# A decoder layer on one core: row stores on another queue, a reordered overflow job, and a score product of full height

## The chip, the cores and the metric

The kernel runs on one core of a Trainium2 chip. A core has TensorE (PE in the profile, with PEld for its weight loads), VectorE (DVE), ScalarE (ACT), GpSimd (POOL) and SyncE (SP), which computes nothing here and issues DMAs. Each of SP, ACT and POOL issues the DMAs of its own queue in program order; the transfers run on the core's 16 DMA engines. The metric is the time of one launch in device microseconds.

## The reference

The kernel computes one layer of a hybrid decoder trunk for 1024 tokens of width 1024, in float32. Two branches (a gated linear recurrence, and attention with a compressed key and value latent) read one combined projection; they are merged by gates, pass an output product and are added to the residual. Then a router chooses for each token one of eight groups and two of the eight experts in it, and the experts' outputs, weighted, are added to the residual. Cut to the two places that the change touches:

```python
# attention, per head: key and query have 128 plain and 64 rotary dimensions
k = rmsnorm(concat([k_nope, k_pe]), qk_k_g);  q = rmsnorm(q, qk_q_g)
q, k = rope on the last 64 dimensions
for s0 in range(0, 1024, 128):                      # blocks of 128 queries, causal
    s = einsum("bqhd,bkhd->bhqk", q[:, s0:e], k[:, :e]) * scale
    o = softmax(mask(s)) @ v[:, :e]
# experts
h = x + merged @ w_out
expert, gate = top 2 of the experts in the best group of rmsnorm(h) @ router
y[token] += gate * ((silu(u @ w1[e]) * (u @ w3[e])) @ w2[e])     # 64 experts, D_EXPERT 256
out = h + y
```

## The kernel before

The work runs in stages, all on one core: the input products (to about 590 us of the profile), attention by heads (591 to 898), the two branch products and the merge (898 to 985), the output product with the router (985 to 1128), and the experts (1128 to the end).

**Attention.** Products are made from float32 numbers that are split into a high and a low part. `head_T` makes the transposed, split queries and keys of a head (`qnh`, `qnl`, `knh`, `knl` for the 128 plain dimensions; `qpe`, `kph`, `kpl` for the rotary ones), in tiles of two buffers each. In `qpe`, rows 0 to 63 hold the high part of the rotary query and rows 64 to 127 the low part; `kph` holds the rotary key's high part over the same 128 rows; `kpl` holds its low part in rows 0 to 63 alone. `attn_a` makes the scores of one block of 128 queries in groups of five products (L691) into one PSUM bank: `knh` by `qnh`, `knl` by `qnh`, `knh` by `qnl`, `kph` by `qpe`, all of 128 rows, and `kpl` by `qpe` of 64 rows. A block has one group, or two where more than 512 keys are in reach. VectorE then adds the mask and takes the extreme of each row (L695), ScalarE takes the exponential (L700), PE transposes the probabilities (L718) and multiplies them by the values (L119, L120). GpSimd makes the rotated parts of the next head (L625 to L643) and some of the low parts (L116).

**Output product and router.** `product` multiplies one block of 128 tokens by the output weights, which lie split in eight tiles `wo0` to `wo7` (L989). `route` adds the residual, stores the rows to two tensors in memory (`xs_d` at L1009, `out` at L1010; 512 KB each), both issued by SP, makes the router's logits (L1035) and the position of each token in a table, and scatters two sets of rows into that table, `tab_d`, by indirect DMAs of GpSimd (L1123). There are eight blocks. The table holds 128 places for each of 32 tiles, and one load brings it back as `rec_all` (L1156, SP).

**Experts.** A tile `t` is two experts of 64 places each. `gather` fetches its rows from `xs_d` (L1198, GpSimd), `select` transposes them (L1233), `gemm1` makes the two hidden products (L1271), `turn` and `gemm2` the last one (L1284, L1298), `gather_out` and `scatter` add it to `out` (L1216, L1223). The weights come in chunks of 1 MB, six a tile, through a ring of 19 buffers that `wchunk` hands out in order: five `c` and four `m`, which stand on space that is free from the merge on, and ten `w` (`w9` to `w18`), which stand where the output weights and the router's tiles were. `load` issues the chunks on SP (L1247), two tiles ahead. The row indices of tile 0 are made ahead of the table's return (`first_tile`), so its gather waits for no table load.

**The overflow job.** Places beyond an expert's 64 are computed in jobs of one expert and 64 rows. One job is always run among the tiles, as a generator that the tile loop steps on: the first `next(job)` issues three chunks (L1392) and a gather (L1395), the second makes the hidden products (L1405), the third turns them (L1413), the fourth makes the last product (L1424) and the scatter. With `JI = 6` these steps stand in the program at tiles 6, 7, 8 (behind that tile's `load`) and at the end of tile 9. A scheduler may move instructions against the order in which the program is written, within what tiles and buffers allow.

Of the kernel before, what the change touches and what calls it, by code (L numbers as in the profile page):

```python
# [43 lines left out]
JI = 6  # L44
# [7 lines left out]
def block_kernel(ctx, tc, x, positions, norm1_g, w_in, conv_w, conv_b, lru_wa, lru_ba, lru_wx,  # L52
# [3 lines left out]
    nc = tc.nc  # L56
# [502 lines left out]
    with pool_of(name="hd", bufs=2) as hd, \  # L559
# [86 lines left out]
        def head_T(pr, j, hf, which):  # L646
            if ("t", j) not in pr:
                pr["t", j] = {nm: hd.tile([128, S], F32R, name=nm)
                              for nm in ("qnh", "qnl", "knh", "knl", "qpe", "kph", "kpl")}
            t = pr["t", j]  # L650
            qs, ks = pr["qs"], pr["ks"]
            qp, kp = pr["qk", j, hf]
            s_ = slice(hf * 512, hf * 512 + 512)
            pt = tps.tile([128, 4, 128], F32, name="tp")
            for q in range(4):
                tb = hf * 4 + q
                src = (qs[:, tb, j, 0:DN], ks[:, tb, j], qp[:, q].rearrange("p a b -> p (a b)"),
                       kp[:, q].rearrange("p a b -> p (a b)"))[which]
                nc.tensor.transpose(pt[:, q], src, ident)
            pt = pt.rearrange("p a b -> p (a b)")  # L660
            if which < 2:
                a, b = (("qnh", "qnl"), ("knh", "knl"))[which]
                gcol = pch[:, 64 + which:65 + which]
                nc.scalar.activation(t[a][:, s_], pt, AF.Copy, scale=gcol)
                nc.vector.scalar_tensor_tensor(t[b][:, s_], pt, gcol, f32v(t[a][:, s_]),
                                               op0=ALU.mult, op1=ALU.subtract)
            elif which == 2:
                hi_of(t["qpe"][:, s_], pt)
                lo_of(t["qpe"][64:128, s_], pt[64:128], t["qpe"][64:128, s_], nc.vector)
            else:  # L670
                hi_of(t["kph"][:, s_], pt)
                lo_of(t["kpl"][0:64, s_], pt[0:64], t["kph"][0:64, s_], nc.vector)
# [4 lines left out]
        def attn_a(h, qb):  # L677
# [8 lines left out]
            for ch in range(nw):  # L686
                cc = slice(ch * w, ch * w + w)
                for n, (a, b, r) in enumerate((("qnh", "knh", 128), ("qnh", "knl", 128),
                                               ("qnl", "knh", 128), ("qpe", "kph", 128),
                                               ("qpe", "kpl", 64))):  # L690
                    nc.tensor.matmul(psv[:, ch], t[a][0:r, qsl], t[b][0:r, cc],  # L691
                                     start=n == 0, stop=n == 4)

# [252 lines left out]
    with pool_of(name="xe", bufs=1, side="right") as xe, \  # L946
# [45 lines left out]
        def route(tb):  # L992
# [11 lines left out]
            for hf in range(2):  # L1004
# [1 line left out]
                nc.vector.tensor_tensor(xt[:, s_], xt[:, s_], px[:, s_], op=ALU.add)  # L1006
                junk = wo.tile([128, 512], BF16, name="junk", bufs=2)
                nc.scalar.activation(junk, xt[:, s_], AF.Square, accum_out=ss[:, hf:hf + 1])
            nc.sync.dma_start(xs_d[tsl, :], xt)  # L1009
            nc.sync.dma_start(out[tsl, :], xt)  # L1010
            nc.vector.tensor_tensor(ss[:, 0:1], ss[:, 0:1], ss[:, 1:2], op=ALU.add)
            rec = rp.tile([128, 2, 4], F32, name="rec", bufs=4)
            nc.vector.memset(rec, 0.0)
# [106 lines left out]
            for j in range(2):  # L1120
                pos = rp.tile([128, 1], I32, name=f"pos{j}", bufs=4)
                nc.vector.tensor_copy(pos, ps_[:, j:j + 1])
                nc.gpsimd.indirect_dma_start(  # L1123
                    out=tab_d, out_offset=bass.IndirectOffsetOnAxis(ap=pos, axis=0),
                    in_=rec[:, j], in_offset=None, bounds_check=128 * NT_ - 1, oob_is_err=False)

        for tb in range(NB):
            product(tb, 0)
# [7 lines left out]
        for _ in route(NB - 1):  # L1136
# [16 lines left out]
    onef = eg.tile([128, 64], F32, name="onef")  # L1153
    nc.gpsimd.memset(onef, 1.0)
    rec_all = eg.tile([128, NT_, 4], F32, name="rec_all")
    nc.sync.dma_start(rec_all.rearrange("p a c -> p (a c)"),  # L1156
                      tab_d.rearrange("(p a) c -> p (a c)", p=128))
    toki = eg.tile([128, NT_], I32, name="toki")
    nc.vector.tensor_copy(toki, rec_all[:, :, 0])
# [52 lines left out]
    def gather_out(t):  # L1212
        xo = rows_("xo")
        if t < 3:
            nc.gpsimd.memset(xo, 0.0)
        unordered(nc.gpsimd.indirect_dma_start(  # L1216
            out=xo, out_offset=None, in_=out,
            in_offset=bass.IndirectOffsetOnAxis(ap=tok_of(t), axis=0),
            bounds_check=S - 1, oob_is_err=False), t)
        st["xo", t] = xo  # L1220
# [216 lines left out]
    for t in range(NT_):  # L1437
        if t == 1:
            job_table()
            jrec, ji = job_rec(eg, cps, const, "kro")  # L1440
            job = job_run(jrec, ji, eg, wchunk, (cps, hps, tps2, yps), ("c", "ph", "pt", "py"),
                          rows_)
        if t + 2 < NT_:
            gather(t + 2)
        if t:
            gather_out(t - 1)
        if 3 <= t + 2 < NT_ - 1:
            load(t + 2, (w1_r, w3_r, w2_r))
        elif t + 2 == NT_ - 1:
            load(t + 2, (w1_r, w3_r))  # L1450
            for hf in range(2):
                load_2h(t + 2, hf)
        if JI <= t < JI + 3:
            next(job)
        gemm1(t)
        if t + 1 < NT_:
            select(t + 1)
        if t:
            turn(t - 1)
            gemm2(t - 1)  # L1460
            scatter(t - 1)
        if t == JI + 3:

            next(job)
    gather_out(NT_ - 1)
# [51 lines left out]
```

## Time and profile before

| | before |
|---|---|
| median of 3 runs (least to most) | 1696.21 us (1695.99 to 1697.54) |
| profiled execution, whole | 1698.7 us |
| its span | 1696.9 us |
| PE busy | 1527.0 us, 90% |
| DVE, ACT, POOL busy | 715.5, 499.0, 459.7 us |
| read from memory, written | 307.74 MB, 48.59 MB |

The time outside the span is 1.8 us. PE's share of 90% is an average over stages: it is nearly full in the input products, in attention and in the output product, while in the experts' stage the DMA engines are nearly full and PE has gaps. So each stage has to be read by itself, and the views below are all cut by stretch, line or engine. A matmul's duration in the profile is longer than its distance to the next one, since matmuls are pipelined; what a product costs in a row of products is read from the start times.

### The profile page before, as it was taken

How to read it: one execution, taken by the hardware profiler on the slowest of the kernel's cores; microseconds unless marked ns; L12 is line 12 of the kernel's file. 1: busy time of each engine (PE TensorE's matmuls, PEld its weight loads, DVE VectorE, ACT ScalarE, POOL GpSimd, SP SyncE). 2: the span in 40 equal slices, each digit the busy share in tenths (PEclk: the TensorE clock that was granted, in tenths of full speed). 3: DMA queues.
4: the chain of work that ended last, by engine and by line, in shares of the span. 5: the costliest groups of instructions: out<-in, count | busy, mean ns of one | idle time of the engine just before them, and what ended most of it. 6: DMA issues, size and time to landing. Idle time of an engine off the chain costs nothing. (4 is left out here: it accounts for less than half of the span.)

```text
span 1696.9 us, 22297 instructions
## 1 busy us (share of the span) xinstructions
PE 1527.0 (90%) x8484; PEld 1141.5 (67%) x8484; DVE 715.5 (42%) x1806; ACT 499.0 (29%) x1088; POOL 459.7 (27%) x456
## 2 busy tenths in 40 slices
PE   5999998999999999999998999979739879878776
PEld 5988886888888877878777878856416445444443
DVE  7744646420012777777875346644102222112111
ACT  5325464631112466666553112210000000000000
POOL 4034343321223235252603411232200221211111
PEclk9999999999999999999999999989869999999999
DMA  5212212353345201010206674349997999999995
GB/s 189 61 53 64 64 59 62 100 186 100 99 157 168 78 8 38 10 38 25 76 16 212 194 261 161 114 187 417 418 413 295 418 417 417 413 406 412 404 415 199
DMA packets 129489, 331.89 MB, mean 196 GB/s; under 512 B 16315, under 2 KB 81413, under 8 KB 104677
## 3 DMA queue, kind: packets, MB, share of 16 engines
q1 hardware_dynamic: 113844, 304.02, 47.7%
q0 software_dynamic: 14816, 25.57, 4.1%
q8 instruction: 68, 1.11, 0.3%
q10 hardware_dynamic: 720, 0.85, 0.2%
q14 instruction: 41, 0.33, 0.1%
HBM read 307.74 MB, written 48.59 MB: 210 GB/s over the span
## 5 line engine op out<-in xcount | busy, mean ns | idle before, releaser
L116 POOL TENSOR_TENSOR w_lo<-w_raw,w_hi 128x1024 fp32r<-128x1024 f32 x40 | 97.6, 2440 | 266.2 <-ACT w_hi L113 266.1
L1271 PE MATMUL ph<-w,x 128*64 128x256 f32 x992 | 140.2, 395 | 19.6 <-DMA w<-in_exp_w_dram 19.5
L259 PE MATMUL pp<-uTh,w_hi 128*128 128x512 f32 x496 | 156.3, 396 | 1.1 <-ACT xp L368 1.1
L262 PE MATMUL pp<-uTl,w_hi 128*128 128x512 f32 x496 | 155.8, 395 | 0.0
L265 PE MATMUL pp<-uTh,w_lo 128*128 128x512 f32 x496 | 155.7, 395 | 0.0
L1234 DVE TENSOR_TENSOR x<-c,g2col 128x512 f32<-128x512 f32 (+1 forms) x66 | 44.0, 677 | 246.5 <-PE ph L1271 193.3
L1261 ACT ACTIVATE hs<-ph,rec_all 128x256 f32<-128x256 f32 x31 | 14.7, 474 | 424.7 <-PE ph L1271 424.7
L1271 PEld LDWEIGHTS ph<-w,x 128*64 128x64 f32 x992 | 83.4, 142 | 63.4 <-DMA w<-in_exp_w_dram 26.1
L259 PEld LDWEIGHTS pp<-uTh,w_hi 128*128 128x128 f32 x496 | 93.3, 188 | 23.6 <-ACT xp L368 1.1
L262 PEld LDWEIGHTS pp<-uTl,w_hi 128*128 128x128 f32 x496 | 93.3, 188 | 22.7
L265 PEld LDWEIGHTS pp<-uTh,w_lo 128*128 128x128 f32 x496 | 93.1, 188 | 22.6
L1301 DVE SCALAR_TENSOR_TENSOR xo<-py,rec_all,xo 128x512 f32<-128x512 f32 x62 | 46.5, 751 | 144.4 <-PE py L1298 128.1
L1216 POOL DMA_INDIRECT xo<-out_dram,toki x31 | 31.6, 1019 | 275.1 <-DMA out_dram<-xo,toki 247.8
L989 PE MATMUL px<-wo,ms 128*128 128x512 f32 x384 | 94.3, 399 | 1.0 <-DVE ms L116 1.0
L1271 PE MATMUL ph<-c,x 128*64 128x256 f32 x592 | 84.2, 385 | 5.9 <-DMA c<-in_exp_w_dram 5.1
L1233 PE MATMUL c<-ident,x 128*128 128x128 f32 (+1 forms) x264 | 50.0, 307 | 41.5 <-DVE x L1234 14.9
L1233 PEld LDWEIGHTS c<-ident,x 128*128 128x128 f32 (+1 forms) x264 | 35.7, 194 | 73.7 <-issue 36.1
L113 ACT ACTIVATE w_hi<-w_raw 128x1024 fp32r<-128x1024 f32 x40 | 42.1, 1053 | 139.6 <-PE pp L262 113.3
L989 PEld LDWEIGHTS px<-wo,ms 128*128 128x128 f32 x384 | 70.5, 188 | 17.0 <-DVE ms L116 1.4
L1298 PE MATMUL py<-w,hT 128*64 128x512 f32 x280 | 75.0, 623 | 4.8 <-issue 2.1
L1271 PE MATMUL ph<-m,x 128*64 128x256 f32 x464 | 70.4, 386 | 6.5 <-DMA m<-in_exp_w_dram 6.5
L116 DVE TENSOR_TENSOR cTl<-gt,cTh 128x1024 fp32r<-128x1024 f32 x4 | 4.9, 1226 | 165.2 <-ACT cTh L113 165.2
(640 smaller groups left out, 3402.5 us busy)
## 6 DMA issues: line engine op xcount, KB each, us to landing
w<-in_exp_w_dram SPq DMA_DIRECT2D x100, 1024.0 KB, 23.6
c<-in_exp_w_dram SPq DMA_DIRECT2D x53, 1024.0 KB, 24.0
m<-in_exp_w_dram SPq DMA_DIRECT2D x40, 1024.0 KB, 21.9
w_raw<-in_w_in_dram SPq DMA_DIRECT2D x32, 512.0 KB, 5.3
xt<-in_x_dram SPq DMA_DIRECT2D x8, 512.0 KB, 5.4
hg_d<-hh SPq DMA_DIRECT2D x8, 512.0 KB, 2.6
gt<-hg_d SPq DMA_DIRECT2D x8, 512.0 KB
sgb_d<-gt SPq DMA_DIRECT2D x8, 512.0 KB, 5.1
```

The lines of the kernel that those rows point to most:

```text
L113: nc.scalar.activation(dst, src, AF.Copy)
L116: eng.tensor_tensor(dst, src, f32v(hi), op=ALU.subtract)
L259: nc.tensor.matmul(ps[:, s_], wh[:, k], ah[:, k, s_], start=k == 0, stop=False)
L262: nc.tensor.matmul(ps[:, s_], wh[:, k], al[:, k, s_], start=False, stop=False)
L265: nc.tensor.matmul(ps[:, s_], wl[:, k], ah[:, k, s_], start=False, stop=k == KD - 1)
L989: nc.tensor.matmul(px[:, s_], ms[:, a, k], wos[k][:, b, s_], start=k == 0 and a + b == 0, stop=k == KD - 1 and a == 1)
L1216: unordered(nc.gpsimd.indirect_dma_start(out=xo, out_offset=None, in_=out, in_offset=bass.IndirectOffsetOnAxis(ap=tok_of(t), axis=0), boun ...
L1233: nc.tensor.transpose(pt[:, kk, 0:n], x_r[:, hf * 4 + kk], ident[0:n, 0:n])
L1234: nc.vector.tensor_tensor(xT[:, hf * 4:hf * 4 + 4, 0:n], pt[:, :, 0:n], g2col[:, hf * 4:hf * 4 + 4, None].to_broadcast([128, 4, n]), op=AL ...
L1271: nc.tensor.matmul(ph[64 * j:64 * j + 64, wi * 256:wi * 256 + 256], xT[:, k, 64 * j:64 * j + 64], w[2 * wi + j][:, k * 256:k * 256 + 256], ...
L1298: nc.tensor.matmul(py[64 * j:64 * j + 64], hT[:, kk, 64 * j:64 * j + 64], w2[j][:, o_:o_ + 512], start=kk == 0, stop=kk == 1)
L1301: nc.vector.scalar_tensor_tensor(xo[:, s_], py, rec_of(t, 1), xo[:, s_], op0=ALU.mult, op1=ALU.add)
```

## The change

It has four parts. The rotary key's low part `kpl` gets a second half of zeros, written by a GpSimd memset when the tile is made (eight memsets in all), and its product uses 128 rows. The row stores of `route` are issued by ScalarE, and the table load by GpSimd. The table's scatters are declared independent of each other. The overflow job's steps stand elsewhere: the first ahead of `load(8)`, the others at tiles 8, 9 and the end of 10.

```diff
@@ head_T
                               for nm in ("qnh", "qnl", "knh", "knl", "qpe", "kph", "kpl")}
+
+                nc.gpsimd.memset(f32v(pr["t", j]["kpl"][64:128]), 0.0)
@@ attn_a
-                                               ("qpe", "kpl", 64))):
+                                               ("qpe", "kpl", 128))):
@@ route
-            nc.sync.dma_start(xs_d[tsl, :], xt)
-            nc.sync.dma_start(out[tsl, :], xt)
+            nc.scalar.dma_start(xs_d[tsl, :], xt)
+            nc.scalar.dma_start(out[tsl, :], xt)
...
-                nc.gpsimd.indirect_dma_start(
+                sc = nc.gpsimd.indirect_dma_start(
                     out=tab_d, out_offset=bass.IndirectOffsetOnAxis(ap=pos, axis=0),
                     in_=rec[:, j], in_offset=None, bounds_check=128 * NT_ - 1, oob_is_err=False)
+                for o in blk.setdefault("tab", []):
+                    tc.declare_no_dep(sc.ins, o.ins, reason="each pair has a row of its own")
+                blk["tab"].append(sc)
@@ the table's load
-    nc.sync.dma_start(rec_all.rearrange("p a c -> p (a c)"),
+    nc.gpsimd.dma_start(rec_all.rearrange("p a c -> p (a c)"),
                       tab_d.rearrange("(p a) c -> p (a c)", p=128))
@@ the tile loop
+        if t == JI:
+            next(job)
         if 3 <= t + 2 < NT_ - 1:
             load(t + 2, (w1_r, w3_r, w2_r))
...
-        if JI <= t < JI + 3:
+        if t in (JI + 2, JI + 3):
             next(job)
         gemm1(t)
...
-        if t == JI + 3:
+        if t == JI + 4:
             next(job)
```

SP's queue at the end of the router, before (`x` is a block's residual rows; `c`, `m` and `w` are weight chunks; line numbers of the changed kernel are five higher there):

```order
L1009 DMA xs_d<-x_9854 128x1024
L1010 DMA out_dram<-x_9854 128x1024
L1247 DMA m_10689<-in_exp_w_dram 128x2048
L1009 DMA xs_d<-x_10039 128x1024
L1010 DMA out_dram<-x_10039 128x1024
L1009 DMA xs_d<-x_10224 128x1024
L1010 DMA out_dram<-x_10224 128x1024
L1156 DMA rec_all<-tab_d 128x128
L1247 DMA w_10691<-in_exp_w_dram 128x2048
L1247 DMA w_10693<-in_exp_w_dram 128x2048
```

and now:

```order
L975 DMA x_9862<-in_x_dram 128x1024
L1252 DMA m_10695<-in_exp_w_dram 128x2048
L975 DMA x_10047<-in_x_dram 128x1024
L975 DMA x_10232<-in_x_dram 128x1024
L1252 DMA m_10697<-in_exp_w_dram 128x2048
L1252 DMA w_10699<-in_exp_w_dram 128x2048
L1252 DMA w_10701<-in_exp_w_dram 128x2048
```

No row store and no table load stands ahead of the chunks `w9` to `w18` on SP any more.

GpSimd's queue at the same place, before (`x_10663` and `x_10668` are the rows of tiles 0 and 1, `xo` the rows that the tiles' outputs are added to):

```order
L1123 DMA tab_d<-rec,pos_10404 4096x4
L1197 MEMSET x_10668 128x1024
L1123 DMA tab_d<-rec,pos_10618 4096x4
L1198 DMA x_10663<-xs_d,tok_9019 128x1024
L1123 DMA tab_d<-rec,pos_10623 4096x4
L1154 MEMSET onef 128x64
L1215 MEMSET xo_10885 128x1024
L1215 MEMSET xo_10975 128x1024
L1216 DMA xo_10885<-out_dram,tok_9019 128x1024
L1198 DMA x_10668<-xs_d,toki 128x1024
```

and now:

```order
L1125 DMA tab_d<-rec,pos_10412 4096x4
L1202 MEMSET x_10676 128x1024
L1125 DMA tab_d<-rec,pos_10626 4096x4
L1125 DMA tab_d<-rec,pos_10631 4096x4
L1203 DMA x_10671<-xs_d,tok_9027 128x1024
L1159 MEMSET onef 128x64
L1161 DMA rec_all<-tab_d 128x128
L1220 MEMSET xo_10893 128x1024
L1220 MEMSET xo_10983 128x1024
L1221 DMA xo_10893<-out_dram,tok_9027 128x1024
L1203 DMA x_10676<-xs_d,toki 128x1024
```

The gather of tile 0 now stands behind both scatters of the last block, and the table load stands between it and the gather of tile 1.

PE around the overflow job, before (L1298 is `gemm2` of tile 6, L1405 the job's hidden products, L1271 `gemm1` of tile 7, then of tile 8):

```order
L1298 MATMUL py<-c_11167,hT 64x512
L1298 MATMUL py<-c_11169,hT 64x512
...
L1405 MATMUL ph<-w_11358,x_11457 64x256 x8
L1405 MATMUL ph<-w_11360,x_11457 64x256 x8
L1271 MATMUL ph<-c_11248,x_11404 64x256
L1271 MATMUL ph<-m_11250,x_11404 64x256
...
L1413 MATMUL pt<-ident,jhs 128x64 x2
L1233 MATMUL c<-ident,x_11437 128x128 x4
L1271 MATMUL ph<-w_11337,x_11526 64x256
```

and now (L1276 is `gemm1` of tile 7 at the top and of tile 8 at the foot, L1303 `gemm2` of tile 7, L1410 the job's hidden products):

```order
L1276 MATMUL ph<-m_11260,x_11412 64x256
L1276 MATMUL ph<-m_11262,x_11412 64x256
...
L1303 MATMUL py<-m_11264,hT 64x512
L1303 MATMUL py<-w_11266,hT 64x512
...
L1410 MATMUL ph<-w_11354,x_11554 64x256 x8
L1410 MATMUL ph<-w_11356,x_11554 64x256 x8
L1238 MATMUL c<-ident,x_11534 128x128 x4
L1418 MATMUL pt<-ident,jhs 128x64 x2
L1238 MATMUL c<-ident,x_11656 128x128 x3
L1276 MATMUL ph<-w_11364,x_11501 64x256
```

Before, the job's chunks were loaded behind those of tile 8, and its products stood ahead of tile 7's; now the chunks are loaded ahead of tile 8's, and the products stand between tiles 7 and 8, as the chunks do in SP's queue.

## Rows read from the trace of the kernel before

**Rows 1.** Windows: us, busy time of each engine (instructions), clock, DMA share, GB/s.

```profile
591.00:700.00 109.00, 106.64 (x620) 85.90 (x619) 84.51 (x211) 70.28 (x210) 41.72 (x67) 1.00 0.08 27
1500.00:1600.00 100.00, 79.45 (x506) 42.34 (x502) 16.13 (x26) 4.51 (x11) 18.17 (x18) 0.97 1.01 410
```

**Rows 2.** Timeline of PE in attention: start, length, instruction, names, partitions by columns.

```profile
862.46 0.40 PE L691 MATMUL s<-knh,qnl 128*128 128x512 f32 x1
862.69 0.39 PE L691 MATMUL s<-kph,qpe 128*128 128x512 f32 x1
863.01 0.49 PE L691 MATMUL s<-kpl,qpe 64*128 64x512 f32 x1
863.43 0.88 PE L718 MATMUL tp<-ident,P 128*128 128x128 f32 x6
```

**Rows 3.** Timeline of PE's weight loads in the same stretch; in brackets idle time and cause.

```profile
862.46 0.19 PEld L691 LDWEIGHTS s<-kph,qpe 128*128 128x128 f32 x1
863.01 0.18 PEld L691 LDWEIGHTS s<-kpl,qpe 64*128 64x128 f32 x1 [0.36 <-issue]
863.43 0.64 PEld L718 LDWEIGHTS tp<-ident,P 128*128 128x128 f32 x6 [0.24 <-issue]
```

**Rows 4.** Waits in 591 to 898: engine, line, cause: total us, times, longest.

```profile
POOL xg L634 <- DVE qs L593: 59.1, 5, 24.8
PEld s L691 <- issue: 28.1, 112, 0.4
ACT pth L113 <- PE tp L718: 27.8, 36, 2.5
PEld tp L718 <- issue: 5.2, 24, 0.3
```

**Rows 5.** Line L691: count, least, median, longest ns, first and last start, forms.

```profile
L691 PE MATMUL s<-kpl,qpe x96: 322/441/632, 594.6 to 897.6; 64*128 64x512 f32 x24, 64*128 64x384 f32 x24, 64*128 64x448 f32 x16, 64*128 64x320 f32 x16
```

**Rows 6.** Timeline of SP from the router's end on.

```profile
1127.54 0.32 SPq L1156 DMA_DIRECT2D rec_all<-tab_d  x1
1127.92 10.25 SPq L1247 DMA_DIRECT2D w<-in_exp_w_dram  x10
...
1159.73 5.69 SPq L1247 DMA_DIRECT2D m<-in_exp_w_dram  x4
```

**Rows 7.** Timeline of GpSimd at the router's end.

```profile
1118.19 0.97 POOL L1197 MEMSET x<- 128x1024 f32 x1
1121.74 0.97 POOL L1123 DMA_INDIRECT tab_d<-rec,pos  x1 [2.58 <-DVE pos L1122]
1123.25 1.05 POOL L1198 DMA_INDIRECT x<-xs_d,tok  x1 [0.54 <-issue]
1124.61 1.03 POOL L1123 DMA_INDIRECT tab_d<-rec,pos  x1 [0.31 <-issue]
```

**Rows 8.** Timeline of PE from the last output products to tile 1.

```profile
1100.20 8.17 PE L989 MATMUL px<-wo,ms 128*128 128x512 f32 x34
...
1129.02 8.13 PE L1271 MATMUL ph<-c,x 128*64 128x256 f32 x64
1140.63 1.46 PE L1233 MATMUL c<-ident,x 128*128 128x128 f32 x8 [3.48 <-DMA x<-xs_d,toki]
```

**Rows 9.** DMA issues in 1100 to 1180: count, KB, median us from issue to landing.

```profile
m<-in_exp_w_dram SPq DMA_DIRECT2D x4, 1024.0 KB, 23.0
...
x<-xs_d,toki POOLq DMA_INDIRECT x7, 11.4
...
x<-xs_d,tok POOLq DMA_INDIRECT x1, 4.0
```

**Rows 10.** DMA rates in 1230 to 1310, forty slices of 2 us.

```profile
GB/s 420 412 397 432 426 418 422 406 428 414 414 418 414 426 422 414 430 414 434 393 344 344 254 193 123 53 115 397 426 422 418 418 82 0 57 352 369 408 434 418
```

**Rows 11.** Timeline of SP around the overflow job.

```profile
1256.13 26.24 SPq L1247 DMA_DIRECT2D c<-in_exp_w_dram  x5
```

**Rows 12.** Timeline of PE at the job's first products.

```profile
1268.52 9.82 PE L1405 MATMUL ph<-w,x 128*64 128x256 f32 x31 [26.17 <-DMA w<-in_exp_w_dram]
```

## The prediction

> **What bounds the kernel now.** I read the windows first, to see which engine is full in which stretch. In the first part of attention PE is busy 106.64 of 109 us, DVE 84.51 and ACT 70.28, at full clock, with the DMA engines nearly idle [rows 1]: attention is PE's. In 1500 to 1600 PE is busy 79.45 of 100 us, while the DMA share is 1.01 at 410 GB/s [rows 1]: there the stream of expert weights sets the pace. So a microsecond that attention loses or gains moves all later stages, and in the experts only that counts which lets the chunk stream start earlier or run without a hole. Next I read timelines: PE and its weight loads inside one score group [rows 2, 3], then SP, GpSimd and PE where the experts begin [rows 6 to 8], and last the DMA rates around the overflow job, where the full stream has holes [rows 10].
>
> **Part 1, the fifth score product.** The reader should look at start times, not durations. At 512 columns `knh` starts at 862.46 and `kph` at 862.69, 0.23 us apart; from `kph` to `kpl` it is 0.32, and from `kpl` to what follows 0.42 [rows 2]. Against 0.23 each, one 64-row product costs 0.09 + 0.19 = 0.28 us more than a product of full height. The weight loads say why: the load for `kpl` starts with its product, at 863.01, after 0.36 us of idle time put down to "issue", and the next load starts with its product too, after 0.24 [rows 3], while the load for `kph` starts at 862.46, 0.23 us ahead of its product. Around the 64-row product nothing is loaded ahead. There are 96 of these products, of 512 columns down to 128 [rows 5]; the extra is a switch's and not the columns', so I take it for all alike: 96 x 0.28 = 27 us. The waits give nearly the same by another way: the weight loads of L691 sat idle 28.1 us for "issue" [rows 4]. Adding the 5.2 us before the transposes that follow [rows 4] gives 33, the upper end. What could eat the gain is the other engines: ACT waits 27.8 us for PE's transposes [rows 4] and DVE has 24 us free of 109 in the first stretch [rows 1], so both have room for most of it; the lower end, 15, is about half, for places where the chain from scores to probabilities and back ends last.
>
> [...]
>
> The eight memsets are GpSimd's. A memset of the same columns on all partitions took 0.97 us [rows 7], so 8 us of GpSimd at most, beside an engine that is busy 41.72 of 109 us [rows 1] and waits 59.1 us in five long stretches of up to 24.8 for DVE [rows 4]. I cost them at nothing. Each must wait for the last product that read the same buffer two heads before, which by then is over or nearly; if that cover is gone, the rotation of the next head stands behind it (the slower rival).
>
> **Part 2, the queues at the experts' start.** Before, the table load is issued at 1127.54 and the first of ten chunks at 1127.92 [rows 6]. What these chunks need in memory on the chip is free when the last output products are over, at 1100.20 + 8.17 = 1108.4 [rows 8]. Now they are issued there, 19.5 us earlier; at 410 GB/s [rows 1] 1 MB takes 2.6 us, so ten are in by about 1134. The whole 19.5 does not reach the end, because the ring is then full: the next chunks wait for `gemm1` and `gemm2` of tile 0. Before, the chunks that these release found a backlog: the four `m` of 1159.73 to 1165.4 landed 23.0 us after their issue [rows 6, 9], their middle at about 1185.5. Now there is no backlog; their middle lands about four chunks, with the gathers between them 2.9 us each, behind the end of `gemm2(0)`.
>
> That end moves too. GpSimd issues the gather of tile 0 behind both scatters, at about 1124.6 instead of 1123.25 [rows 7], and into a loaded stream: gathers took 4.0 us in the idle one and 11.4 in the full one [rows 9]. I take 8.5, since the early chunks are nearly in, so it lands at 1133 instead of 1127.2, 6 us late. Of this 3.5 come back, as PE waited so long for the gather of tile 1 [rows 8], which now has time. `gemm2(0)`, which the issue at 1159.73 followed at once [rows 6], then ends near 1162 instead of 1159.5, and the middle of the `m` chunks lands at 1162 + 4 x 2.9 + 2 = 1175.5, against 1185.5: 10 us. Bounds: with a gather of 4.0 us about 15; with one of 11.4 us that also starts some 10 late, behind the memset that must wait for the last row stores, a loss of 5. The two issues a block on ACT are free: ACT is hardly used there and they took 0.3 to 0.4 us each on SP's queue (the table load's 0.32 in [rows 6]).
>
> [...]
>
> **Part 3, the overflow job.** Before, PE reaches the job's products and stands 26.17 us for their chunks [rows 12]; these were queued behind tile 8's, while tile 7's products, which would free buffers, stand behind the job. So the five `c` chunks take 26.24 us to issue [rows 11], and the DMA rate falls: over slices 20 to 27 the shortfall against 418 GB/s is 7.3 us, and in slices 33 to 38 5.9 [rows 10], 13 together by the mean over 16 engines. [...] What all lost are the slices with next to nothing (82, 0 and 57: 5.3 us, and a little of 53). I take 6. After the change the order of loads and products agrees, so PE has no reason to wait longer for the job than for a tile. The job's last chunk keeps its buffer until the end of tile 10, one tile longer; the chunk that needs this buffer comes 19 chunks later (over 50 us), and the hold decides only if PE is more than some 8 us behind the stream. Bounds: 11 gained, 10 lost.
>
> **Sum.** 27 + 10 + 6 = 43 us. The profiled execution took 1698.7 us, so it would take 1655.7; it stood 2.5 us above the median 1696.2, so the median forecast is 1653. The stages between (branch products, output product) keep their length and start 27 us earlier.
>
> **Rivals.**
> - Attention pays half: with PE faster, the chain of DVE's mask, ACT's exponential and the split ends last in many blocks. For it: DVE at 84.51 of 109 us; against it: ACT waits for PE, and PE hardly for anyone. 27 becomes 14: 1666.
> - Row count does not matter: the fifth product stays as slow at 128 rows, because something else (its place as the last of a group) holds the loads back. Against it: the `issue` gap stands ahead of the 64-row load and behind it, and not inside the group. Only parts 2 and 3 are left: 1680.
> - The experts' start gives nothing: the gather of tile 0 comes 12 us later instead of 6, or the queue had been no obstacle. 1663, and with its loss of 5, 1668.
> - The job leaves its hole, or moves it to where its last chunk's buffer is needed at tile 11: 1659, or with a new hole of 10 us 1669.
> - Slower: the memset is the next head's first access to `kpl`, and it stands in GpSimd's order amid the rotation of queries and keys. If it waits for a product of two heads before that is not over, the rotation, the transposes and PE wait. To outweigh 43 us it must cost PE 43 / 8 = 5.4 us at each of the eight tiles; below 5.4 the kernel is still faster. Doubled, 10.8, it gives 1653 + 86 = 1739; at 6 us, 1701. Against it: two buffers, and waits of up to 24.8 us in which it can lie [rows 4].
>
> **Chances.** Forecast, all three near their size: 0.50. Attention half: 0.16. Row count without effect: 0.06. Experts' start without gain: 0.16. Job: 0.08. Slower: 0.04. Of the forecast's own size the range is about 1643 to 1661. The cases to 1668 belong in the 8 of 10, and a few microseconds below 1643 for terms at their upper ends (33 + 15 + 11 = 59 gives 1637): 1638 to 1674. A change of 0.2%, 3.4 us, is about what a measurement of this kernel tells from none. Only the slower rival, or several bad ends at once, come near it: faster 0.95, within 0.2% 0.02, slower 0.03.
>
> **What would show it.** Part 1: in the new timeline of PE the five products of a group start 0.23 us apart, the "issue" idle time of the weight loads at L693 falls from 28.1 to a few us, and attention ends about 27 us earlier. Part 2: the first `w` chunk is issued at the end of the last output product and not 19 us behind it; gather 0 lands 6 us later relative to that end, and the `m` chunks behind `gemm2(0)` land within some 10 us of issue. Part 3: no slice under 300 GB/s between tiles 6 and 12, and no wait of 26 us ahead of the job's products. I would be wrong if PE's waits for DVE or ACT in attention rise by over 10 us, if the stream has holes after 1165 of the present time axis, or if GpSimd is found waiting at a memset of `kpl` with PE idle behind it.

## Result and the profile after

The changed kernel takes 1680.36 us (median of 4 runs, 1678.57 to 1681.56) beside 1696.66 us of the kernel before (4 runs, 1695.99 to 1697.54): a ratio of 0.9903, 95% interval 0.9886 to 0.992. That is 16.3 us saved where 43 were forecast; 1680 lies outside the range of 1638 to 1674. The profiled execution took 1680.37 us with a span of 1678.6.

The windows, as in [rows 1]:

```profile
591.00:700.00 109.00, 100.78 (x625) 90.34 (x626) 86.58 (x211) 70.58 (x210) 43.87 (x69) 0.97 0.08 27
1500.00:1600.00 100.00, 79.52 (x522) 43.78 (x521) 17.59 (x28) 5.16 (x12) 16.25 (x16) 0.97 1.01 411
```

In attention PE is now idle 8 us of 109 (2.4 before), does five more instructions in that time, and its clock is no longer full (0.97 for 1.00). The stream of the experts is as it was. From the first to the last score product attention takes 296.2 us, against 306.5: 10 us less, not 27. Five more of the profiles below have attention as the change has it, with PE's products in the same order; in them it takes 293.4 to 295.9 us. So the gain is 10 to 13 us, and a difference of 3 us between two profiles is no sign of anything.

**The fifth product itself.** One score group of 384 columns on PE, and the weight loads beside it, as in [rows 2, 3]:

```profile
847.73 0.34 PE L693 MATMUL s<-knh,qnl 128*128 128x384 f32 x1
847.91 0.33 PE L693 MATMUL s<-kph,qpe 128*128 128x384 f32 x1
848.08 0.34 PE L693 MATMUL s<-kpl,qpe 128*128 128x384 f32 x1
848.26 1.03 PE L720 MATMUL tp<-ident,P 128*128 128x128 f32 x8
```

```profile
847.91 0.19 PEld L693 LDWEIGHTS s<-kpl,qpe 128*128 128x128 f32 x1
848.09 0.97 PEld L720 LDWEIGHTS tp<-ident,P 128*128 128x128 f32 x8
```

All starts are 0.17 to 0.18 us apart, before the fifth product and behind it, and its weights load while the fourth runs. Over all 96 groups the median distance into the fifth product fell by 0.09 us, and that out of it by 0.19, as [rows 2] had it. The duration by form, least, median and longest, fell from the 322/441/632 of [rows 5] to

```profile
L693 PE MATMUL s<-kpl,qpe x96: 273/340/522, 594.1 to 886.9; 128*128 128x512 f32 x24, 128*128 128x384 f32 x24, 128*128 128x448 f32 x16, 128*128 128x320 f32 x16
```

The 28.1 us of idle time for "issue" in [rows 4] are gone. Here is attention as one window, from the first score product to the last, before and then after:

```profile
591.40:897.95 306.55, 298.64 (x1740) 239.84 (x1741) 230.85 (x591) 189.49 (x560) 113.46 (x171) 0.99 0.10 33
```

```profile
590.90:887.20 296.30, 274.62 (x1742) 245.64 (x1743) 233.01 (x591) 189.71 (x560) 120.01 (x178) 0.98 0.10 34
```

PE's busy time fell by 24.0 us, but its idle time rose from 7.9 to 21.7: 13.8 us came back as waits. One wait was longer than 0.9 us before; now there are seven. Added up by who ended them, PE's waits for DVE rose from 5.2 to 16.0 us, those for ACT from 2.1 to 4.7. In 591 to 888 the waits read (engine, line, cause: total us, times, longest):

```profile
PEld tp L120 <- DVE ptl L116: 12.5, 13, 4.8
PEld tp L119 <- ACT pth L113: 12.2, 26, 2.1
ACT pth L113 <- PE tp L720: 10.9, 18, 1.5
PE tp L120 <- DVE ptl L116: 9.1, 9, 4.5
```

ACT's wait for PE's transposes fell from 27.8 [rows 4] to 10.9: this slack was used. In its place PE waits 9.1 us for the lower parts of the probabilities, which DVE makes; in the kernel before these two lines of `ptl` read 5.0 and 3.3. The longest such wait, with DVE's, ACT's and GpSimd's timelines ahead of it:

```profile
804.96 2.31 DVE L106 TENSOR_TENSOR rs_t<-rs_t,rs_v 128x16 f32<-128x16 f32 x1
807.20 0.15 DVE L704 RECIPROCAL sm<-sm 128x1 f32<-128x1 f32 x1
807.31 2.27 DVE L108 SCALAR_TENSOR_TENSOR rs_y<-rs_t,rs_i 128x16 f32<-128x16 f32 x1
...
810.59 1.28 DVE L697 CUSTOM_DVE_ANT_0 s<-s,mask,rr__5963 128x1024 f32<-128x1024 f32 x1
...
811.80 0.42 DVE L116 TENSOR_TENSOR ptl<-tp,pth 128x256 fp32r<-128x256 f32 x1
```

```profile
806.02 0.38 ACT L113 ACTIVATE pth<-tp 128x256 fp32r<-128x256 f32 x1
```

```profile
804.86 2.38 POOL L116 TENSOR_TENSOR w<-c,w 128x1024 fp32r<-128x1024 f32 x1
807.21 2.33 POOL L116 TENSOR_TENSOR c<-c,c 128x1024 fp32r<-128x1024 f32 x1
```

```profile
812.27 0.58 PE L120 MATMUL tp<-ptl,vh 128*128 128x256 f32 x1 [4.55 <-DVE ptl L116]
...
813.77 0.47 PE L693 MATMUL s<-kph,qpe 128*128 128x320 f32 x1
814.04 0.47 PE L693 MATMUL s<-kpl,qpe 128*128 128x320 f32 x1
...
872.01 0.31 PE L693 MATMUL s<-kph,qpe 128*128 128x320 f32 x1
872.16 0.31 PE L693 MATMUL s<-kpl,qpe 128*128 128x320 f32 x1
```

and the window behind it:

```profile
811.80:818.60 6.80, 6.33 (x26) 6.29 (x27) 5.00 (x15) 6.15 (x11) 5.80 (x5) 0.50 0.19 69
```

Read upwards: PE stands 4.55 us for one `ptl`. What `ptl` is made from, ACT's `pth`, is there from 806.4 on, but DVE works almost without a break from 802.9 to 812.9, and `ptl` stands in its queue behind a mask and the steps of an inverse square root for the next heads. Two of these steps, which elsewhere take 0.17 us on 16 columns, last 2.31 and 2.27 us and end together with GpSimd's subtraction of 1024 columns. After the wait PE goes on at half pace for a while: 0.27 us from product to product at 320 columns, against 0.15 at 872. The granted clock says why: 0.50 from 811.8 to 818.6, against 1.00 at 872. In all it stood at this level for 13.6 us of attention, in three stretches that begin in or just behind a wait of PE (1.35, 1.86 and 4.55 us), against 3.4 us before, behind a wait of 2.74. By an estimate, half of the 10.2 us more, some 5 us were lost so; they are part of the busy time above.

**The experts' start.** SP and ACT, then GpSimd and PE, as in [rows 6 to 8]:

```profile
1096.89 27.25 SPq L1252 DMA_DIRECT2D w<-in_exp_w_dram  x10
...
1156.25 1.98 SPq L1252 DMA_DIRECT2D m<-in_exp_w_dram  x4
```

```profile
1101.42 0.33 ACTq L1011 DMA_DIRECT2D xs_d<-x  x1
1101.79 0.57 ACTq L1012 DMA_DIRECT2D out_dram<-x  x1
```

```profile
1115.08 0.95 POOL L1202 MEMSET x<- 128x1024 f32 x1 [10.08 <-DMA out_dram<-x]
1116.18 0.98 POOL L1125 DMA_INDIRECT tab_d<-rec,pos  x1 [0.16 <-issue]
1117.47 0.97 POOL L1125 DMA_INDIRECT tab_d<-rec,pos  x1 [0.30 <-issue]
1118.75 1.05 POOL L1203 DMA_INDIRECT x<-xs_d,tok  x1 [0.30 <-issue]
```

```profile
1126.73 1.95 PE L1238 MATMUL c<-ident,x 128*128 128x128 f32 x8 [12.40 <-DMA x<-xs_d,tok]
```

The first chunk leaves 31 us earlier (22.4 when counted from the issue of the last row stores, where 19.5 were forecast). But the last row stores, issued at 1101.42 and 1101.79, travel among ten chunks and land at 1110.85 and 1114.85; before they took 5 to 6 us. GpSimd stands 10.08 us at the memset for them, and both scatters and the gather of tile 0 stand behind it. Counted from the last row stores' issue, the gather lands 25.2 us later (17.2 before), and tile 0's second products end 5.1 us later than before. In return the `m` chunks behind them land 12.9 us after issue, not 23.0 [rows 9]:

```profile
m<-in_exp_w_dram SPq DMA_DIRECT2D x4, 1024.0 KB, 12.9
...
x<-xs_d,tok POOLq DMA_INDIRECT x1, 7.8
```

**The overflow job.** The DMA rates in 1230 to 1310, SP and PE, as in [rows 10 to 12]:

```profile
GB/s 406 446 403 418 420 410 426 426 401 428 408 416 414 426 418 426 414 426 410 414 412 432 416 408 414 391 363 361 287 211 205 76 109 66 438 406 428 418 446 408
```

```profile
1264.05 35.49 SPq L1252 DMA_DIRECT2D w<-in_exp_w_dram  x10
```

```profile
1247.06 7.07 PE L1410 MATMUL ph<-w,x 128*64 128x256 f32 x32
...
1291.96 1.07 PE L1429 MATMUL py<-w,jhT 128*64 128x512 f32 x2
```

PE no longer waits 26 us ahead of the job's products. One hole is left instead of two, 8.1 us against 13 by the prediction's count (the shortfall against 418 GB/s): among the ten chunks of 1264.05 one needs the buffer of the job's second weights; it is issued at 1296.07, right behind the job's last product (1291.96 to 1296.0).

### The profile page after: what moved, and what is told of

Its sections match the earlier page's. It is cut to its first block, busy times and chain, and to the rows that moved or that the text cites. A ratio compares the mean times of both kernels' runs of the same rounds, so it can differ in the third digit from the quotient of the medians.

```text
span 1678.6 us, 22322 instructions
## 1 busy us (share of the span) xinstructions
PE 1509.7 (90%) x8484; PEld 1143.6 (68%) x8484; DVE 721.9 (43%) x1806; ACT 500.0 (30%) x1088; POOL 468.7 (28%) x465
## 5 line engine op out<-in xcount | busy, mean ns | idle before, releaser
L1276 PE MATMUL ph<-w,x 128*64 128x256 f32 x992 | 143.7, 400 | 22.6 <-DMA w<-in_exp_w_dram 22.5
L1266 ACT ACTIVATE hs<-ph,rec_all 128x256 f32<-128x256 f32 x31 | 14.7, 476 | 436.3 <-PE ph L1276 436.3
L1276 PEld LDWEIGHTS ph<-w,x 128*64 128x64 f32 x992 | 84.2, 144 | 70.1 <-DMA w<-in_exp_w_dram 30.3
L1276 PE MATMUL ph<-c,x 128*64 128x256 f32 x592 | 88.2, 400 | 12.1 <-DMA c<-in_exp_w_dram 10.2
L1238 PE MATMUL c<-ident,x 128*128 128x128 f32 (+1 forms) x264 | 53.8, 315 | 46.2 <-DVE x L1239 24.6
L991 PEld LDWEIGHTS px<-wo,ms 128*128 128x128 f32 x384 | 70.0, 188 | 16.3 <-DVE ms L116 1.4
L1276 PE MATMUL ph<-m,x 128*64 128x256 f32 x464 | 72.4, 392 | 9.1 <-DMA m<-in_exp_w_dram 9.0
L1303 PE MATMUL py<-w,hT 128*64 128x512 f32 x280 | 75.8, 643 | 2.7 <-ACT hT L1291 1.4
L1276 PEld LDWEIGHTS ph<-c,x 128*64 128x64 f32 x592 | 51.7, 144 | 38.9 <-DMA c<-in_exp_w_dram 13.7
```

Source lines behind the costliest of these rows:

```text
L991: nc.tensor.matmul(px[:, s_], ms[:, a, k], wos[k][:, b, s_], start=k == 0 and a + b == 0, stop=k == KD - 1 and a == 1)
L1238: nc.tensor.transpose(pt[:, kk, 0:n], x_r[:, hf * 4 + kk], ident[0:n, 0:n])
L1276: nc.tensor.matmul(ph[64 * j:64 * j + 64, wi * 256:wi * 256 + 256], xT[:, k, 64 * j:64 * j + 64], w[2 * wi + j][:, k * 256:k * 256 + 256], ...
L1303: nc.tensor.matmul(py[64 * j:64 * j + 64], hT[:, kk, 64 * j:64 * j + 64], w2[j][:, o_:o_ + 512], start=kk == 0, stop=kk == 1)
```

## The experiments

Each is named by its edit. Times of before differ from set to set (1695.87 to 1698.63 us), so the ratio counts. The lowest and the highest time of one kernel stand 1.5 to 10 us apart. "Theory A" and the rivals are those of the expectation that stands above each result.

**Each part alone.** Part 1 alone is the first two pieces of the diff (memset and 128 rows):

```
+ nc.gpsimd.memset(f32v(pr["t", j]["kpl"][64:128]), 0.0)
- ("qpe", "kpl", 64)
+ ("qpe", "kpl", 128)
```

> The kernel before with part 1 alone (kpl filled to 128 rows, eight memsets). Theory A: the fifth product gets faster by the whole 0.25 to 0.28 us, but PE then waits for the chain of mask, exponential and split on DVE and ACT, as in the full change: first to last score product 296 us instead of 306, and 1687 us in all (9 to 10 less than before). Rival: the other two parts take away what attention gave, and alone it gives 27 us: 1670. Rival: all of the full change's 16 us come from attention: 1680.

Measured: 1686.78 us, ratio 0.9942 (0.9925 to 0.9958), 9.9 us less: theory A. Attention took 294.5 us, 12 less than before. The loss of part 1 is attention's own and not a collision with the other parts.

Part 2 alone (row stores on ACT, table load on GpSimd, scatters unordered among themselves):

```
- nc.sync.dma_start(xs_d[tsl, :], xt)
+ nc.scalar.dma_start(xs_d[tsl, :], xt)
- nc.sync.dma_start(rec_all...
+ nc.gpsimd.dma_start(rec_all...
```

> The kernel before with part 2 alone (row stores on ScalarE, table load on GpSimd, scatters independent). Theory A: the first chunks are issued at the end of the output product, the gather of tile 0 comes 7 to 8 us late, and the chunks behind the end of tile 0 land 7 to 8 us earlier against the output product's end: 1689 us. Forecast's size: 1687. Rival: a queue was no obstacle, nothing gained: 1697.

Measured: 1693.74 us (10 runs, 1690.07 to 1698.66), ratio 0.9984 (0.9973 to 0.9996), 3.0 us less. It lies between theory A and no gain; 10 us is excluded. The traced run was one of the two fastest, and in it the first `m` chunk behind `gemm2(0)` lands 5.3 us earlier than before, counted from the issue of the last row stores; why the median run keeps only 3.0 of that stays open.

Part 3 alone (the job's loads and products in the queue's order):

```
+ if t == JI: next(job)
- if JI <= t < JI + 3:
+ if t in (JI + 2, JI + 3):
- if t == JI + 3:
+ if t == JI + 4:
```

> The kernel before with part 3 alone (the job's steps in the queue's order). Theory A: PE no longer stands 26 us ahead of the job's products, but the job's last chunk holds its buffer to the end of tile 10 while PE is behind the stream, so the hole moves to the chunk that needs this buffer and half of the gain goes: 2 to 3 us less than before, 1694. Forecast's size: 1691. Rival: the move is a loss, as the stream waits longer at the new place: 1698.

Measured: 1691.52 us (8 runs), ratio 0.9969 (0.9958 to 0.9979), 5.2 us less: the forecast's size. The hole is shallower here than in the change (no slice under 250 GB/s, against 66); why is not shown. Added up, the three give 18.1 us, the change 16.3.

**A shorter chain.** The multiply that normalises the probabilities is left out of both kernels:

```
- nc.vector.tensor_scalar(P[:, 0:e], P[:, 0:e], sm, None, op0=ALU.mult)
```

> The kernel before without the multiply that normalises the probabilities on VectorE (64 instructions; the output is therefore not the reference's); only attention's length is read. From the first to the last score product it took 306.4 us with the multiply. Theory A (the chain from scores to probabilities on VectorE and ScalarE ends last in part of the blocks even before the change): some 300 us. Rival B (attention is TensorE's alone before the change): 305 to 307.

> The changed kernel without the same multiply (64 instructions of VectorE left out). With it the fifth product at 128 rows shortened attention by 10 us, though the distances between products add up to 24.9. Theory A (what the products gain is lost again where the chain over VectorE and ScalarE ends last): with the chain shorter, attention is 20 to 25 us shorter than in the run of the kernel before without the multiply. Rival B (the distances gain nothing more because TensorE itself is slower elsewhere, at a lower clock or behind the memsets): the difference stays at 8 to 12 us.

Attention's length is read from the first product of the groups by form (count, least, median, longest ns, first and last start), before and after:

```profile
L691 PE MATMUL s<-knh,qnh x96: 282/422/667, 592.9 to 895.1; 128*128 128x512 f32 x24, 128*128 128x384 f32 x24, 128*128 128x448 f32 x16, 128*128 128x320 f32 x16
```

```profile
L693 PE MATMUL s<-knh,qnh x96: 221/392/500, 591.3 to 873.5; 128*128 128x512 f32 x24, 128*128 128x384 f32 x24, 128*128 128x448 f32 x16, 128*128 128x320 f32 x16
```

To the end of the last product that is 303.2 and 283.0 us. Without the multiply part 1 is worth 20.2 us, with it 10 to 13: theory A. And the multiply itself cost the kernel before 3.3 us, the changed one 10 to 13: DVE's work between a score group and its next use had been nearly hidden behind PE, and now it is what PE waits for in places. PE's waits for DVE agree: 3.1 and 8.4 us in this pair, 5.2 and 16.0 in the pair with the multiply. The clock was low for 6.8 us in both of the pair, so it has no part in the 20.2. PE's order differs from that of the kernels with the multiply, but is the same for both of the pair; each is one run. The expectation's 24.9 us is a sum of distances between products; PE's busy time, read above, fell by 24.0. The pair can't part two causes, as the multiply both lengthens the chain from scores to probabilities and fills DVE's queue; in the longest wait above it was the queue.

**The memsets twice and four times.**

```
+ for _ in range(2):
      nc.gpsimd.memset(f32v(pr["t", j]["kpl"][64:128]), 0.0)
```

> The changed kernel with each of GpSimd's eight memsets of the rotary key's lower part issued twice: the suspected cost doubled. Theory A (they lie in GpSimd's waits): attention's 296.2 us from the first to the last score product within 1.5 us, and the time within the scatter of 2 us. Rival B (the memsets eat part of what the products gain, up to 0.95 us at each head on the path): attention 4 to 8 us longer, 1684 to 1688.

> The changed kernel with each of GpSimd's eight memsets issued four times. With each twice, attention was 300.1 us in one profile, against 293.4 to 296.2 in six profiles with the same order on TensorE. Theory A (a set of memsets costs attention some 4 to 6 us, since VectorE and the rotation stand beside or behind them): 306 to 314 us in attention, 1690 to 1698 in time. Rival B (the run with two was scatter): attention within 293 to 300, the time 1678 to 1684.

Attention took 300.1 us with two, 304.3 with four; the time 1683.35 us (one run) and 1687.48 (9 runs, ratio 0.9939, 0.9922 to 0.9956). The first misses rival B's bounds by a hair and theory A's by more, the second lies between its two theories; in a row, counted from the change's 296.2 and 1680.36, they show that each further set costs 2 to 4 us. So the forecast's "nothing" for the memsets was wrong by about that much, by extension to the first set, which was not measured by itself. Most of it is lost in the first 22 us, where GpSimd's rotation for the second head is late; with four memsets PE waits there for the rotated queries, and 10 us later for an exponential:

```profile
594.66 0.66 PE L662 MATMUL tp<-ident,qp 128*128 128x128 f32 x4 [1.42 <-POOL qp L643]
...
604.48 0.69 PE L694 MATMUL s<-knh,qnh 128*128 128x384 f32 x1 [2.95 <-ACT P L703]
```

In the change itself one place shows such a cost: beside the memset of `kpl` at 627.60 (0.95 us) a VectorE step that usually takes 0.17 us lasts 0.97, and a wait of PE for VectorE of 1.35 us follows at 628.3. How much of this wait the memset makes is not shown.

**The row stores back on SP**, the table load still on GpSimd's queue:

```
- nc.scalar.dma_start(xs_d[tsl, :], xt)
- nc.scalar.dma_start(out[tsl, :], xt)
+ nc.sync.dma_start(xs_d[tsl, :], xt)
+ nc.sync.dma_start(out[tsl, :], xt)
```

> The changed kernel with the row stores back on SP's queue, the table load still on GpSimd's. Theory A (part 2 loses at the gather of tile 0 what the earlier chunks give: the last row stores travel among ten chunks and land 10 us after issue, and the memset, both scatters and the gather stand behind them): the last stores are issued ahead of the chunks and land in about 4 us, the gather of tile 0 is issued some 6 us earlier, the chunks 4.7 us later; 1675 to 1678 against 1680.4. Rival B (the issue of the first chunk counts): 1684 to 1686. Rival C (neither counts, the ring is full before tile 0 starts): 1680.

Measured: 1676.39 us (1670.17 to 1677.66), ratio 0.9877 (0.9846 to 0.9907), 4 us under the change: theory A by the time, though the gather of tile 0 came forward less than the 6 us that it expected. SP and GpSimd:

```profile
1099.66 0.32 SPq L1011 DMA_DIRECT2D xs_d<-x  x1
1100.04 0.42 SPq L1012 DMA_DIRECT2D out_dram<-x  x1
1100.52 18.30 SPq L1252 DMA_DIRECT2D w<-in_exp_w_dram  x10
```

```profile
1105.74 0.95 POOL L1202 MEMSET x<- 128x1024 f32 x1 [2.40 <-DMA out_dram<-x]
1111.64 0.97 POOL L1125 DMA_INDIRECT tab_d<-rec,pos  x1 [4.95 <-DVE pos L1124]
```

The stores go ahead of the chunks and land in 4.6 and 5.5 us, the memset waits 2.40 us instead of 10.08, and what holds the scatters now is the router itself. The gather is issued 14.6 us behind the stores' issue, against 17.3 in the change. Counted from the stores' issue, the first chunk leaves 5.4 us later than in the change, yet the first `m` chunk lands 3.2 us earlier. A chunk that leaves early into a ring that fills anyway is worth less than a gather on time. The intervals of this run and of the change overlap, so the 4 us rest on the trace as well.

**No memset ahead of the first gathers.**

```
- if t < 3:
-     nc.gpsimd.memset(xg, 0.0)
```

> The changed kernel without the memset that stands ahead of each of the first three gathers (each gather fills all rows that are used). Theory A (GpSimd stands 10 us at this memset, behind the last row stores, and the scatters and the gather of tile 0 stand behind it): gather 0 is issued earlier by 1 to 4 us, since the last scatter needs no store, and 1677 to 1680 result. Rival B (the gather itself must wait for the row stores that it reads): no more than the memset's own time, 1679 to 1681.

Measured: 1677.67 us, ratio 0.9892 (0.9864 to 0.9921). That is in theory A's range; rival B's lower end, 1679, is too near to be excluded. The gather of tile 0 is issued 14.7 us behind the stores' issue (17.3 in the change), within what theory A said, and the scatters wait for the router's positions (8.02 us).

**The job at tile 20** (`JI = 6` becomes `JI = 20`):

> The changed kernel with JI = 20 instead of 6, so that the job runs where PE is ahead of the stream. Theory A: with PE waiting for chunks anyway no buffer is held too long, both holes are gone: 3 to 8 us less than the changed kernel, 1673 to 1677. Rival: the holes cost nothing in the end, because the stream is not what ends last at that place: 1680, no difference.

Measured: 1677.07 us, ratio 0.9882 (0.986 to 0.9903): the edge of theory A's range, though the intervals overlap. But its account, that both holes are gone, is wrong. The DMA rates in 1225 to 1305 have no hole, and those in 1500 to 1580, where the job now stands, have one:

```profile
GB/s 404 418 412 424 426 422 422 416 406 422 412 426 418 414 412 422 420 414 418 438 414 410 414 424 418 399 426 430 410 440 406 391 434 412 422 426 414 426 410 422
```

```profile
GB/s 420 416 426 414 381 307 422 369 401 426 412 420 428 414 272 244 207 234 201 397 418 430 418 420 426 418 412 426 426 422 418 393 424 416 412 416 420 418 424 422
```

The hole went along with the job and is shallower: 4.5 us of shortfall in its five low slices, and none under 200 GB/s, against 8.1 us in the change.

**The three together, and GpSimd's subtractions cut in four.** The three are the row stores on SP, no memset ahead of the first gathers, and the job at tile 20. The cut, shortened (`s_` is a quarter of the columns):

```
- lo_of(t[:, 1], raw, t[:, 0], eng)
+ for c in range(4): lo_of(t[:, 1, s_], raw[:, s_], t[:, 0, s_], eng)
```

> The changed kernel with three edits that each gave 2.7 to 4 us alone: row stores on SP's queue, no memset ahead of the first gathers, the overflow job at tile 20 instead of 6. Theory A: the first two overlap in part (both bring the gather of tile 0 forward), the third adds: 1671 to 1674. Rival B: all three shorten one and the same wait, or the job's 3.3 us was scatter between runs: 1675 to 1678.

> As the run with the three edits, and in attention GpSimd's subtractions of 768 and 1024 columns (1.8 and 2.4 us each) cut into four instructions; the order on every other engine is the same. In the changed kernel small instructions of VectorE that take 0.17 us lasted up to 2.3 us and ended with such a subtraction, 16.3 us together in attention; the largest gap of TensorE (4.55 us) stands behind two of them. Theory A (VectorE is held for the length of GpSimd's instruction): no small VectorE instruction over 0.9 us in attention, attention 3 to 6 us shorter, 3 to 6 us less than without the cuts. Rival B (what is held goes by the columns in all, or those stalls are off the path): attention and time the same within 1.5 us.

Measured: 1671.79 us (ratio 0.9855, 0.9835 to 0.9876), and 1669.12 (0.9828, 0.9809 to 0.9847), in the same set: the best of this study, 28.6 us under before. The first is theory A: 8.6 us under the change, where the three edits alone add up to 10. The second is 2.7 us under the first, just short of theory A's 3, and the intervals overlap. With the cuts DVE's two steps and PE's wait read

```profile
803.53 0.66 DVE L106 TENSOR_TENSOR rs_t<-rs_t,rs_v 128x16 f32<-128x16 f32 x1
804.11 0.15 DVE L710 RECIPROCAL sm<-sm 128x1 f32<-128x1 f32 x1
804.23 0.65 DVE L108 SCALAR_TENSOR_TENSOR rs_y<-rs_t,rs_i 128x16 f32<-128x16 f32 x1
```

```profile
809.59 0.58 PE L120 MATMUL tp<-ptl,vh 128*128 128x256 f32 x1 [3.34 <-DVE ptl L116]
```

The two steps last 0.66 and 0.65 us here; in the change they lasted 2.31 and 2.27 beside GpSimd's subtractions of 2.38 and 2.33. A quarter of those is 0.6, an estimate, so theory A's account of the hold fits. Attention is 3.1 us shorter (290.3 against 293.4), the least that theory A allowed and little more than profiles of one attention differ by; but 290.3 is under all six of them, and of the seven waits over 0.9 us four are left. One small instruction of 0.97 us is left, beside a memset of `kpl`. PE's wait is 3.34 us still: five steps of 16 columns in a row, with one multiply among them, last 0.65 to 0.70 us each (803.53 to 808.00), 3.3 us together, where the same five took 5.1 in the change; how much of the wait is this hold and how much DVE's queue is not shown. The expectation's 16.3 us is too much: in the change's attention only four VectorE steps of this size last over 0.5 us, 6.2 us together.

## Why the prediction was wrong

Of the 27 us that are missing, part 1 lost 17, part 2 lost 7 and part 3 lost 1, by the runs of each part alone; about 2 more are lost where the three meet.

- **Part 1, the distances: right.** 27 us were forecast, 0.28 for each product; the medians fell by 0.09 and 0.19, and PE's busy time in attention fell by 24.0, though some 5 us lost to the lower clock stand in it. The rival that the row count does not matter falls with that. Its time, 1680, is the measured one, but only by chance: part 1, which it left out, gave about what the other two fell short of their forecasts. The weight loads took 0.18 us for 64 rows and 0.19 for 128 [rows 3]; the gain came from when the loads start. That the extra does not go by the columns shows at 384 of them: in the kernel before 0.27 us from the fourth product to the fifth (at 855.01) and 0.37 out of the fifth, in the change 0.17 and 0.18, so 0.10 and 0.19 more, as at 512. By what mechanism a product of 64 rows made the two loads late is not shown; with 128 rows both are early.
- **Part 1, "both have room for most of it": the step that failed.** It was read from totals (24 us of DVE free in 109, ACT waiting 27.8 us). A free share is an average: DVE was busy for some 10 us on end around the longest wait. Each block goes from a score group through DVE, ACT, DVE, PE, ACT and DVE back to PE, with two score buffers to look ahead, and DVE's part of this path was hidden by a margin smaller than the gain: the pair without the multiply shows it. 13.8 us of idle time came back, 10.8 of them as waits for DVE. 10 to 13 us of gain were left, under the lower end of 15. The rival "attention pays half" named the mechanism and was too mild. The sign that the prediction set for this, PE's waits for DVE or ACT up by over 10 us, came true.
- **The memsets at nothing: wrong by some 2 to 4 us** by the runs with two and four. The first set was not measured by itself. That GpSimd waits 59.1 us in five stretches says nothing of the places where the memsets stand, amid the rotation. The slower rival had this mechanism at 5.4 us for each tile; it was real, and less than a tenth of the 43 us that it would have had to outweigh.
- **Part 2, 10 us: mis-sized.** The steps went as listed, but the row stores' own time among the chunks was missing from the forecast's value and stood only in its lower bound: GpSimd waited 10.08 us at the memset. The gather of tile 0 came 8.0 us late instead of 6, tile 0's second products ended 5.1 us late instead of 2.5, and the `m` chunks, which land 16.3 us earlier, owe 8.6 to the stages before and 7.7 to this part, instead of 10; alone the part is worth 3.0 (0.7 to 4.6 by its interval). The rival by which the early issue gives nothing was nearer.
- **Part 3, 6 us: right** (5.2 alone). Of the stated rivals "moves it to where its last chunk's buffer is needed" came true as well: the forecast let the hold decide only where PE is some 8 us behind the stream, and it did decide. The job at tile 20, where the hole is 3.6 us smaller, is 3.3 us faster, though with overlapping intervals. That no slice would be under 300 GB/s was wrong as well: the lowest is 66.

## What to carry to other kernels

A gain on the fullest engine is bounded by the path through the other engines, their queues included, and not by their free shares (here 24.0 us less of PE's busy time gave 10 to 13): follow one item through all engines, compare that time with what the look-ahead covers, and look whether the engines on the path are busy just then. Before small writes move to another queue, ask what they will travel among, and what waits for them; a load that leaves early into a full ring gains little (in the change the first chunk left 22.4 us earlier, and part 2 alone gave 3.0). After a hole in a stream is closed, look at the whole stream: it may only have moved (here 8.1 us of shortfall stood at the new place, for 13). A cheap instruction on an idle engine is free only if it stands outside that engine's own late stretches (here each further set of memsets of 0.95 us cost 2 to 4 us).

## What was not expected of the hardware

Two VectorE instructions of 16 columns lasted about as long as the GpSimd subtraction beside each of them: 2.31 and 2.27 us beside 2.38 and 2.33, where the median of such steps is 0.17. In the kernel before it was two others, 2.31 and 2.30 us (L98 and L99, at 808.46 and 810.80) beside 2.40 and 2.38. With GpSimd's subtractions cut in four the same two of the change lasted 0.66 and 0.65. The two of the change read two tiles, those of the kernel before a single one; the step beside a memset of `kpl` (0.97 us, L99, beside 0.95) reads a single one too, and a memset reads none. What holds VectorE at these places is not shown. What no total shows is that in these runs the length of GpSimd's single instruction set the length of such a stall.
